# Modulation loads issued by GpSimd into three buffers, and twelve output-projection chunks of layer 0 computed in split form

## The chip, the cores and the metric

The kernel runs on one core of a Trainium2 chip. The metric is the device time of one execution in microseconds (us), taken as the median of three runs. TensorE (PE in the profile) multiplies matrices, VectorE (DVE) and ScalarE (ACT) do elementwise work, GpSimd (POOL) does a few small operations, and SyncE (SP) issues the transfers between the memory of the chip (HBM) and the core's own memory (SBUF). TensorE writes into PSUM, a small accumulation memory.

## The reference

A decoder trunk of two layers works on 256 tokens of width 2048, all in float32. Each layer mixes tokens and then applies a gated feed-forward network (FFN). Both are modulated by a vector `c`:

```python
for l in range(DEPTH):                       # DEPTH = 2
    mod = silu(c) @ w_mod[l] + b_mod[l]      # 2048 x 12288 weights, one row of c
    shift1, scale1, gate1, shift2, scale2, gate2 = split(mod, 6)
    h = rms_norm(x, norm1_gain[l]) * (1 + scale1) + shift1
    x = x + gate1 * hybrid_token_mixer(h, ..., w_in[l], ..., w_out[l])
    h = rms_norm(x, norm2_gain[l]) * (1 + scale2) + shift2
    x = x + gate2 * ((silu(h @ w_gate[l]) * (h @ w_up[l])) @ w_down[l])
return rms_norm(x, final_norm_gain)
```

The token mixer multiplies `h` by `w_in` (2048 x 4888 columns), gives the columns to three mixers and multiplies their joined output `mix` (256 x 2048) by `w_out` (2048 x 2048). The three mixers are GLA (gated linear attention, which uses a small 16 x 256 gate weight `w_gk`), a sliding-window attention (SWA) and a gated delta rule (GDN). The FFN is 5632 wide. All weights are read from HBM once, about 600 MB.

## The kernel before

**The large products.** `stream` (L293) walks over jobs. One job is one chunk of 128 rows of a weight matrix and up to 1024 of its columns: SP loads it (L323, 512 KB), and it is multiplied with the transposed activations of both token blocks of 128. A job has one of two forms. In the *whole* form the float32 weights go to TensorE as they are; the profile shows two matmul records for each product of 128x128 with 128x512. In the *split* form ScalarE copies the weights into a rounded part `wh` (L330), VectorE subtracts it to get the rest `wl` (L331), and TensorE does three products: high by high, high by low, low by high (L358). Activations are split too, by `split` (L386). `WHOLE_IN`, `WHOLE_A` and `WHOLE_OUT` say which chunks are whole. `WHOLE_OUT[0] = (0, 1, 2, 3)` makes all four groups of four chunks of layer 0's output projection whole; in layer 1 all are split. Chunk `k` belongs to group `k // 4`: 0 is GLA, 1 and 2 are SWA, 3 is GDN. `to_mix` (L489) puts a mixer's output into tiles of the pool `hm`, and `split_mix` (L520), called ahead of `gla`, splits those groups that are not whole. The output projection runs first over chunks 4 to 15 for both halves of the columns (24 jobs) and then, when GLA is done, over chunks 0 to 3 (8 jobs).

**The modulation.** The products with `c` are not done by TensorE. `mod_segment` (L201) cuts the modulation into segments; a step of one loads 128 rows of `w_mod` by SP (L220), and VectorE multiplies them by one value of `c` for each partition and adds them to an accumulator (L223). Once all steps of a segment are in, `finish` (L228) sums the accumulator over its partitions with TensorE (L238 for gates, L248 for shifts and scales). The first segments, shift1 and scale1 of layer 0 ("early"), are 512 columns wide and land in scratch tiles `g`. All others are 1024 wide: 320 loads of 512 KB into the two buffers `mraw` of the pool `modp`; the two accumulators `acc` are cleared by GpSimd (L212) and get their bias row by a transfer of SP (L213). `finish` of a gate borrows `mraw` buffers as well (L233).

**The order.** `tick` (L273) is called after each job and starts modulation steps at a rate that the constants `RATE_...` set (2.0 steps to a job in layer 0's output projection, 0.4 in its FFN). What the text writes down in this order is then put into one queue for each engine by a scheduler with costs of its own, which pulls work forward where its operands and buffers allow it; each engine runs its queue in order. So a transfer on SP that waits for a buffer holds back all transfers behind it. Other users of GpSimd's queue are `rsqrt` (L408), used by the norms and the mixers, the sinks of SWA (L891), the memsets, and the copy L218, which holds the first modulation load behind the second norm of a layer.

**Small tiles.** `ones` (L163) is a float32 tile of ones that a copy on ScalarE turns into `ones_r` of the type that the fast products use; `ones` itself is used at L594. `load_small` (L464) loads the gate weights `wgk` at the start of each layer, together with other small weights.

## Time and profile before

| what | before |
|---|---|
| median of 3 runs | 2582.44 us (2582.32 to 2587.12) |
| the profiled execution, its own time | 2585.34 us |
| its span, first to last instruction | 2583.5 us |
| busy: TensorE, VectorE, ScalarE, GpSimd | 94%, 66%, 41%, 2% of the span |
| moved by transfers | 600.79 MB, 233 GB/s over the span |
| mean granted TensorE clock | 0.986 of full speed |

The time of the profiled execution is its span and what lies around it. A row of instructions gives the line of the kernel, the engine, the operation, output<-inputs by the program's names, the shapes and the count, then the busy time and the mean duration in ns, then the engine's idle time just before these instructions and what ended it. Matmuls overlap, so that the mean duration of one (some 390 ns) is longer than the step from one to the next. SPq stands for SP's transfer queue. A row of the chain of waits gives the start, the duration and what the chain ran through at that time. `mraw` and `raw` are the buffers of modulation and of weights.

### The profile page before, as it was taken

To read this page: it belongs to the slowest core of one execution; us is meant where nothing else is said; L and a number is where in the kernel's file an instruction comes from. 1 tells how busy PE (TensorE), PEld (TensorE's weight loads), DVE (VectorE), ACT (ScalarE), POOL (GpSimd) and SP (SyncE) were. 2 spreads that over 40 slices of the span, in tenths; PEclk is the share of its full clock that TensorE was granted. 3 is DMA by queue.
4 is the path that set the end of the run, shared out by engine and by line. 5 is a ranking of instruction groups with operands and counts; after the bars stand their busy time and mean duration, and the time that the engine had idled before them with its cause. 6 is when DMAs were issued, how large, how long until landed. Compare 5 with 4: busy or idle time off the path is not lost.

```text
span 2583.5 us, 30803 instructions
## 1 busy us (share of the span) xinstructions
PE 2432.7 (94%) x11164; PEld 1884.1 (73%) x11164; DVE 1714.4 (66%) x2171; ACT 1053.5 (41%) x1548; POOL 58.2 (2%) x117
## 2 busy tenths in 40 slices
PE   4999998889999988999999999999999999999998
PEld 2555785447878767788877878877778878888876
DVE  6767867576675777657578785888664575544555
ACT  2203443124444333344335454564644434344443
POOL 1000000000000000000000000000000000000000
PEclk9999999989999999999999999999999999999999
DMA  9996538777778888868687861675676686666654
GB/s 341 368 322 204 180 114 282 258 231 268 261 259 260 283 268 274 292 193 286 223 277 261 281 192 50 214 232 192 212 256 193 200 286 195 188 191 188 189 184 155
DMA packets 190033, 600.79 MB, mean 233 GB/s; under 512 B 21628, under 2 KB 26268, under 8 KB 189496
## 3 DMA queue, kind: packets, MB, share of 16 engines
q1 hardware_dynamic: 189880, 598.81, 70.7%
q8 instruction: 88, 1.44, 0.2%
q14 instruction: 65, 0.53, 0.1%
HBM read 596.63 MB, written 2.10 MB: 232 GB/s over the span
## 4 chain that ended last, share of the span: by engine, by line
PE 57%; DMA 20%; DVE 10%; issue 8%; ACT 4%; POOL 1%; SPq 1%; DVEq 0%; ACTq 0%; POOLq 0%
PE acc L358 48%; DMA mraw<-in_w_mod 13%; DVE wl L331 4%; DMA raw<-in_w_down 3%; DMA raw<-in_w_in 2%; DVE acc L223 2%; ACT wh L330 1%; PE mm L403 1%; PE ga L895 1%; DMA raw<-in_w_up 1%; PE mm L678 1%; PE mm L685 1%; PE ga L916 1%; DMA raw<-in_w_gate 1%; PE fin L248 1%
## 5 line engine op out<-in xcount | busy, mean ns | idle before, releaser
L358 PE MATMUL acc<-wh,hm 128*128 128x512 f32 (+3 forms) x4872 | 1339.2, 389 | 20.9 <-DVE xs L931 4.7
L330 ACT ACTIVATE wh<-raw 128x1024 fp32r<-128x1024 f32 (+3 forms) x669 | 684.7, 1025 | 985.8 <-PE acc L358 548.9
L331 DVE TENSOR_TENSOR wl<-raw,wh 128x1024 fp32r<-128x1024 f32 (+3 forms) x669 | 785.2, 1179 | 446.6 <-ACT wh L330 444.5
L358 PEld LDWEIGHTS acc<-wh,hm 128*128 128x128 f32 x4872 | 892.0, 189 | 215.8 <-issue 25.5
L358 PE MATMUL acc<-wl,hm 128*128 128x512 f32 (+3 forms) x2484 | 792.3, 394 | 12.2 <-DVE wl L331 9.7
L223 DVE SCALAR_TENSOR_TENSOR acc<-mraw,c_act,acc 128x1024 f32<-128x1024 f32 x320 | 410.3, 1282 | 225.2 <-DMA mraw<-in_w_mod 222.9
L358 PEld LDWEIGHTS acc<-wl,hm 128*128 128x128 f32 x2484 | 458.4, 190 | 124.1 <-DVE wl L331 22.3
L358 PE MATMUL acc<-wh,ahl 128*128 128x512 f32 x560 | 158.4, 397 | 0.0
L358 PEld LDWEIGHTS acc<-wh,ahl 128*128 128x128 f32 x560 | 105.8, 189 | 24.5
L358 PE MATMUL acc<-wl,ahl 128*128 128x512 f32 x280 | 90.8, 398 | 7.2 <-DVE wl L331 7.2
L223 DVE SCALAR_TENSOR_TENSOR g<-g,c_act,g 128x512 f32<-128x512 f32 x128 | 88.7, 747 | 12.6 <-DMA g<-in_w_mod 12.4
L358 PE MATMUL acc<-wh,b 128*128 128x512 f32 (+2 forms) x184 | 74.7, 545 | 2.2 <-ACT b L447 2.1
L358 PE MATMUL acc<-wl,b 128*128 128x512 f32 (+2 forms) x176 | 67.1, 518 | 2.6 <-DVE g L969 2.6
L358 PEld LDWEIGHTS acc<-wl,ahl 128*128 128x128 f32 x280 | 52.2, 189 | 23.1 <-DVE wl L331 11.3
L358 PE MATMUL acc<-raw,b 128*128 128x512 f32 (+2 forms) x176 | 67.6, 524 | 0.0
L358 PEld LDWEIGHTS acc<-wh,b 128*128 128x128 f32 x184 | 35.2, 197 | 30.8 <-issue 23.1
L358 PEld LDWEIGHTS acc<-wl,b 128*128 128x128 f32 x176 | 32.8, 192 | 29.2 <-issue 20.3
L416 ACT ACTIVATE acc<-xs 128x512 f32<-128x512 f32 x32 | 19.0, 595 | 85.7 <-DVE xs L931 85.7
L447 ACT ACTIVATE b<-mm,mod,mod 128x128 f32<-128x128 f32 x24 | 9.2, 461 | 109.7 <-DVE mod L256 92.1
L358 PEld LDWEIGHTS acc<-raw,b 128*128 128x128 f32 x176 | 33.5, 195 | 26.7 <-issue 21.7
L929 DVE TENSOR_TENSOR acc<-acc,gate 128x512 f32<-128x512 f32 x64 | 43.0, 695 | 10.3 <-PE acc L358 10.2
L358 PE MATMUL acc<-raw,hm 128*128 128x512 f32 x88 | 41.7, 598 | 1.4 <-ACT acc L416 1.4
(314 smaller groups left out, 1645.8 us busy)
## 6 DMA issues: line engine op xcount, KB each, us to landing
mraw<-in_w_mod SPq DMA_DIRECT2D x320, 512.0 KB
raw<-in_w_down SPq DMA_DIRECT2D x176, 512.0 KB
raw<-in_w_gate SPq DMA_DIRECT2D x160, 512.0 KB
raw<-in_w_up SPq DMA_DIRECT2D x160, 512.0 KB
raw<-in_w_in SPq DMA_DIRECT2D x72, 512.0 KB
g<-in_w_mod SPq DMA_DIRECT2D x128, 256.0 KB
raw<-in_w_out SPq DMA_DIRECT2D x43, 512.0 KB
raw<-in_w_in SPq DMA_DIRECT2D x32, 264.0 KB
```

The costliest lines, as they stand in the source:

```text
L223: V.scalar_tensor_tensor(acc, raw[:, a], c_act[:, i + a:i + a + 1], acc, ALU.mult, ALU.add)
L248: TE.transpose(ps[:, i * P:(i + 1) * P], acc[:, (j + i) * P:(j + i + 1) * P], ident)
L330: A.activation(wh[:, :width], raw[:, :width], AF.Copy)
L331: V.tensor_tensor(wl[:, :width], raw[:, :width], wh[:, :width].bitcast(F32), ALU.subtract)
L358: TE.matmul(ps[blk, j][:, :segs[j][2]], xa, parts[j][part], start=i == 0 and n == 0, stop=last and n == len(terms) - 1)
L403: TE.transpose(ps[:, j * P:(j + 1) * P], src[:, j * P:(j + 1) * P], ident)
L416: A.activation(scr[0]() if junk is None else junk, xs[:, blk, j * 512:(j + 1) * 512], AF.Square, accum_out=ssq[blk][:, j:j + 1])
L678: TE.matmul(ps[:, s], LT[blk][:, s], Tm[blk][:, s], start=True, stop=True)
L685: TE.matmul(ps[:, s], U[blk][:, s], m1[:, s], start=True, stop=True)
L895: TE.matmul(ps[:, j * nk:(j + 1) * nk], qT[rows, i + j], kT[rows, g, :nk], start=True, stop=True)
L916: TE.matmul(ps[:, j * 64:(j + 1) * 64], pT[:, j * nk + kb * P:j * nk + (kb + 1) * P], kv[kb][:, P + g * 64:P + (g + 1) * 64], start=kb == ...
L929: V.tensor_tensor(ps, ps, need(gate_row, (l, part, j)), ALU.mult)
```

## The change

GpSimd, and no longer SP, issues the bias rows and the loads of the 1024-column modulation segments; the early segments stay with SP. The pool of these loads has three buffers in place of two. In layer 0's output projection the groups 1, 2 and 3 (twelve chunks, 24 jobs) take the split form, and group 0 stays whole. The tile `ones` and the copy that made `ones_r` from it go away: GpSimd writes the ones straight into `ones_r`, and L594 reads that tile as float32. The gate weights are loaded at the start of `gla` into a tile of GLA's own pool.

```diff
-WHOLE_OUT = ((0, 1, 2, 3), ())
+WHOLE_OUT = ((0,), ())
...
-    modp = ctx.enter_context(tc.tile_pool(name="modp", bufs=2))
+    modp = ctx.enter_context(tc.tile_pool(name="modp", bufs=3))
...
-    ones = tl(kp, [P, P], "ones")
-    G.memset(ones, 1.0)
     ones_r = tl(kp, [P, P], "ones_r", F32R)
-    A.activation(ones_r, ones, AF.Copy)
+    G.memset(ones_r.bitcast(F32), 1.0)
...
                 G.memset(st["acc"][:, :width], 0.0)
-                SY.dma_start(st["acc"][0:1, :width], b_mod[l:l + 1, c0:c0 + width])
+                issue = SY if early else G
+                issue.dma_start(st["acc"][0:1, :width], b_mod[l:l + 1, c0:c0 + width])
...
-            SY.dma_start(raw, w_mod[l, i * P:(i + n) * P, c0:c0 + width]
-                         .rearrange("(a p) n -> p a n", p=P))
+            (SY if early else G).dma_start(raw, w_mod[l, i * P:(i + n) * P, c0:c0 + width]
+                                           .rearrange("(a p) n -> p a n", p=P))
...
     def load_small(l):
         small_t[l] = tl(kp, [P, SMALL_W], "small")
         SY.dma_start(small_t[l], small[l][:, 2 * KD:])
-        wgk_t[l] = tl(kp, [16, 256], "wgk")
-        SY.dma_start(wgk_t[l], w_gk[l])
...
                         TE.matmul(ps[:, n:n + 1], sq[:, c, blk * P:(blk + 1) * P],
-                                  ones[:, 0:1], start=True, stop=True)
+                                  ones_r[:, 0:1].bitcast(F32), start=True, stop=True)
...
     def gla(l, pool, qk_tok, v_tok, zg, lr):
 
+        wgk = tl(pool, [16, T], "wgk", bufs=1)
+        SY.dma_start(wgk, w_gk[l])
...
-            TE.matmul(ps[:, blk * T:(blk + 1) * T], lrT[:, blk * P:(blk + 1) * P], wgk_t[l],
+            TE.matmul(ps[:, blk * T:(blk + 1) * T], lrT[:, blk * P:(blk + 1) * P], wgk,
```

More of the change, by code (lines that the diff above doesn't have):

```diff
@@ L458, in trunk @@
     scr = [None, None]
-    small_t, wgk_t = {}, {}
+    small_t = {}
     gains = tl(kp, [P, DEPTH, 2 * KD], "gains")
```

## The prediction

> **What bounds the kernel now.** I read the page first: busy shares, then the chain of waits by engine and by line.
>
> ```profile
> span 2583.5 us, 30803 instructions
> ...
> PE 2432.7 (94%) x11164; PEld 1884.1 (73%) x11164; DVE 1714.4 (66%) x2171; ACT 1053.5 (41%) x1548; POOL 58.2 (2%) x117
> ...
> PE 57%; DMA 20%; DVE 10%; issue 8%; ACT 4%; POOL 1%; SPq 1%; DVEq 0%; ACTq 0%; POOLq 0%
> PE acc L358 48%; DMA mraw<-in_w_mod 13%; DVE wl L331 4%; DMA raw<-in_w_down 3%; DMA raw<-in_w_in 2%; DVE acc L223 2%; ACT wh L330 1%; PE mm L403 1%; PE ga L895 1%; DMA raw<-in_w_up 1%; PE mm L678 1%; PE mm L685 1%; PE ga L916 1%; DMA raw<-in_w_gate 1%; PE fin L248 1%
> ```
>
> TensorE is nearly always busy, and yet 13% of the chain runs through modulation loads. These two fit together only if a busy TensorE is not always a TensorE at full pace, so I next counted its large products in three stretches of the FFNs: layer 0 with modulation, layer 1 with a little of it, layer 1 with none.
>
> ```profile
> 590.00:1100.00 510.00, 478.90 (x2032) 380.58 (x2031) 0.99 0.82 275
> 1850.00:2130.00 280.00, 270.86 (x1177) 219.67 (x1176) 1.00 0.74 238
> 2150.00:2550.00 400.00, 394.79 (x1717) 321.53 (x1717) 1.00 0.61 189
> ```
>
> The columns are the stretch, its length, TensorE's busy time on L358 (records), weight loads, granted clock, transfer share, GB/s. Without modulation the pace is 1717/400 = 4.29 records to a us. At it the 2032 of the first stretch take 473.4 us instead of 510: **36.6 us are lost there**, and 280 - 1177/4.2925 = 5.8 us in the second. The clock is 0.99 to 1.00, so it is not the clock.
>
> What the first stretch waits for is in its groups, its waits on SP, and the chain.
>
> ```profile
> L331 DVE TENSOR_TENSOR wl<-raw,wh 128x1024 fp32r<-128x1024 f32 x170 | 206.1, 1222 | 61.5 <-ACT wh L330 60.9
> L330 ACT ACTIVATE wh<-raw 128x1024 fp32r<-128x1024 f32 x170 | 179.9, 1060 | 295.9 <-PE acc L358 72.9 <-DMA raw<-in_w_down 68.9 <-DMA raw<-in_w_up 65.0
> L223 DVE SCALAR_TENSOR_TENSOR acc<-mraw,c_act,acc 128x1024 f32<-128x1024 f32 x96 | 123.2, 1284 | 95.9 <-DMA mraw<-in_w_mod 95.3
> ```
>
> ```profile
> SPq L323 <- DVE wl L331: 308.8, 161, 4.2
> SPq L220 <- DVE acc L223: 33.7, 30, 2.1
> SPq L220 <- DMA mraw<-in_w_mod: 21.8, 15, 3.0
> ```
>
> There is a ring of waits here. VectorE stands 95.3 us in front of L223, because a modulation load was issued late, behind a weight load that waited for its own buffer (308.8 us on SP). While it stands, `wl` of the next weights waits, their buffer comes free late, and the next weight load is late. The other way round, SP stands 55.5 us (33.7 + 21.8) on modulation loads, with weight loads behind them. One weight load comes every 510/170 = 3.00 us; at full pace it would be 473.4/170 = 2.78.
>
> Before that, layer 0's output projection shows the same in a stronger form.
>
> ```profile
> 481.93 5.50 DMA mraw<-in_w_mod
> 487.46 1.30 DVE acc L223
> ...
> 511.26 4.29 DMA mraw<-in_w_mod
> 515.65 1.30 DVE acc L223
> 517.08 1.09 PE fin L248 x4
> ...
> 521.50 20.97 PE acc L358 x48
> ```
>
> ```profile
> 517.08 1.09 PE L248 MATMUL fin<-consts,acc 128*128 128x128 f32 x4 [5.88 <-DVE acc L223]
> ```
>
> From 481.93 to 517.08 the chain alternates between a load and L223. Its links start 6.8, 4.9, 6.0, 6.6 and 5.0 us apart, the first at 481.93 and the last at 511.26: 29.3 us for five, 5.9 us for a link. A link is two loads, since there are two buffers: 2.9 us for one load. TensorE runs ahead and then stands 5.88 us. After that whole products run without a gap: 20.97/48 = 0.437 us for a record.
>
> **The change part by part.**
>
> *GpSimd's queue and the third buffer, in the FFNs.* The wait of VectorE (95.3 us, 0.56 us for each of 170 weight loads) and the hold on SP (55.5 us, 0.33 us) both lie in the cycle of a weight buffer, and there are three of those. Taking both away shortens the period by (0.56 + 0.33)/3 = 0.30 us, more than the 0.22 us that are there to be had. So the bound is 36.6 us. I take three quarters of it, 27 us, since the loads still share the transfers (0.82 of their time in use at 275 GB/s), and 4 of the 5.8 us in layer 1. What is late next is the weight load itself.
>
> *The split of twelve chunks.* A whole job has 8 records of 0.437 us: 3.50 us. A split one has 12 products, and their step comes from a gapless piece of the chain:
>
> ```profile
> 1112.83 50.38 PE acc L358 x222
> ```
>
> That is 0.227 us each, 2.72 us a job, 0.77 us saved; 24 jobs give 18.5 us, and the stall of 5.88 us can go too: 24.4 us at most. Against it stand VectorE's new work, 24 times 1.22 us (L331) and six tiles in `split_mix` like this row,
>
> ```profile
> L338 DVE TENSOR_TENSOR hm<-raw,hm 128x512 fp32r<-128x512 f32 x32 | 20.9, 688 | 10.8 <-ACT hm L337 10.7
> ```
>
> 29.3 + 4.1 = 33.4 us, and what VectorE has there now:
>
> ```profile
> 393.00:556.00 163.00, 147.16 (x558) 77.27 (x559) 110.49 (x147) 34.91 (x74) 5.89 (x5) 0.98 0.82 272
> ```
>
> ```profile
> L223 DVE SCALAR_TENSOR_TENSOR acc<-mraw,c_act,acc 128x1024 f32<-128x1024 f32 x48 | 61.6, 1282 | 40.9 <-DMA mraw<-in_w_mod 40.7
> ```
>
> (third column: VectorE 110.49 us, fourth: ScalarE 34.91.) 110.5 + 33.4 = 143.9 of 163 us: it fits only because the third buffer takes away most of the 40.7 us of waiting. With GLA's chain of small steps in the same stretch I let it fill to 94%: 143.9/0.94 = 153 us, so 10 us are won. The bounds are a gain of 24.4 us and a loss of 8 (rival 3). ScalarE gets 24 times 1.06 and six times some 0.6 us on 34.91 in 163; that is hidden by its idle time. A whole weight lands in one of nine buffers (`raw`, `wh`, `wl` in turn), a split one in one of three; this cover goes, and the weights of this stage become as exposed as those of the FFN.
>
> *Layer 1's input projection* has both kinds of load as well:
>
> ```profile
> ACT wh L330 <- DMA raw<-in_w_in: 40.8, 28, 5.2
> DVE acc L223 <- DMA mraw<-in_w_mod: 12.9, 14, 1.8
> ```
>
> (1380 to 1500 us.) The wait for weights is the larger one and the transfers have no room for it; of the 12.9 us I take 3 (bounds 0 and 12.9).
>
> *What GpSimd's queue costs.* No transfer of GpSimd is in this trace. Its issue lies between what SP takes and the longest instruction that GpSimd has:
>
> ```profile
> L220 SPq DMA_DIRECT2D mraw<-in_w_mod x320: 327/328/1439, 160.9 to 2122.4; - x160
> ```
>
> ```profile
> L408 POOL TENSOR_TENSOR grs<-gss,half 128x4 f32<-128x4 f32 x8 | 11.3, 1418 | 159.8 <-DVE gss L508 159.8
> L408 POOL TENSOR_TENSOR qkrs<-qkss,half 128x16 f32<-128x16 f32 x2 | 5.8, 2920 | 167.7 <-DVE qkss L596 167.7
> ```
>
> 0.33 us to 2.92 us; I take 1 us, nearer to the short end, since no data passes through GpSimd. A load that lands 0.7 us later than before is covered by the third buffer: it is asked for one period (2.9 us in the fastest stage) sooner. But GpSimd now waits in order for the L223 that frees the buffer, with the memset of the next accumulator, the sinks of SWA (L891) and `rsqrt` behind it; for these wait VectorE's steps in the mixers and norms. The ten rows above and the four norms inside the layers, 14 places, may each come one issue late: 14 times 0.33 is 4.6, times 2.92 is 41; mixers run beside other products, so I take 4 us.
>
> *Small edits.* The gate weights move past the weight loads on SP to the start of GLA, with no queue but SP's to pass. They are needed at the second of these:
>
> ```profile
> 405.27 0.60 PE L747 MATMUL ga<-consts,hm 128*128 128x128 f32 x4
> ...
> 412.32 1.13 PE L761 MATMUL ga<-wgk,lrT 16*128 16x256 f32 x4
> ```
>
> 7 us after GLA's first step; a load of 512 KB takes 3.5 to 5.5 us (chain above), so these 7 us hide a 16 KB one. Without the cover it costs a load, 5.5 us at most, in each layer. The memset in place of memset and copy lies ahead of the first products, behind the first loads: nothing.
>
> *The sum:* -27 - 4 - 10 - 3 + 4 = **-40 us**. The profiled execution took 2585.34 us with a span of 2583.5; it would take 2545.3, with a span of 2543.5. It lies 2.9 us above the median of the runs shown, 2582.44, so against that I predict 2542.
>
> **The rivals.**
>
> *1. The transfers set the pace anyway.* All loads go through the same 16 engines, in use for 0.82 of the time with modulation and 0.61 without. If a weight load is late because the engines are full, a second queue only swaps the order. Against it: 18% of their time is free while VectorE waits. Then the FFN gives 5 us, the output projection 5 and GpSimd costs 4: 2576. The Trainium skill speaks for this one (DMA: Bandwidth & Descriptors, Issuing engines are not separate DMA queues): issuing from several engines only saves the time of issuing. By it alone, the gain would be next to nothing; what it leaves out is one queue waiting for a buffer with the other's work behind it, which the 55.5 us show here.
>
> *2. Slower: weights lose the queue to modulation.* On one queue a weight load waits only for what was issued before it. With two, a modulation load issued after it takes half of the engines while both are under way. One load at the stage's rate takes 0.524 MB / (275/0.82 GB/s) = 1.56 us. The cycle of a weight buffer was to become 0.89 us shorter (0.56 + 0.33), so this decides from 0.89 us on; weights that land a full load later make the period (1.56 - 0.89)/3 = 0.22 us longer, and 170 of them 38 us. With no gain elsewhere and the 4 us for GpSimd: 2624. Against it: at most three modulation loads can be under way, and their rate is set by the program.
>
> *3. VectorE becomes the bound in layer 0's output projection.* If the transfers still make it wait, 33.4 us of new work meet a free time of 163 - 110.5 - 40.7 = 11.8, and 21.6 us do not fit. If the third buffer takes back a third of the wait, 13.6 us, then 8 us are lost instead of 10 won: 2560.
>
> *4. GpSimd is slow to issue.* At 2.92 us a load the three buffers give (5.9 + 2.92)/3 = 2.94 us for one, where two buffers now give 2.9: nothing is won in the output projection; FFN 13 us, less 8 for `rsqrt`: 2577. The Trainium skill warns of it (SBUF — State Buffer, SBUF: two separate sides): GpSimd cannot write the descriptors of its transfers while VectorE runs a copy or the like that uses both its port pairs, so that 0.62 us become 3.1; by its figures a load behind such an instruction comes 2.5 us later. VectorE's main rows here, L331 and L223, have two inputs each and are not of that kind; by the page such a lock would concern little here but this row and its likes:
>
> ```profile
> L441 DVE TENSOR_SCALAR s<-xs,rms 128x512 f32<-128x512 f32 x16 | 7.5, 481 | 0.8 <-POOL rms L408 0.7
> ```
>
> **How the numbers follow.** The forecast gets 0.48, rival 1 0.15, rival 2 0.13, rival 3 0.14, rival 4 0.10. A measurement of this kernel can tell about 0.2%, 5 us, from no change. Forecast and rival 3 are faster; rivals 1 and 4 lie at the edge of that, half of 1 and 0.03 of 4 beyond it; rival 2 is slower, with 0.03 of rival 4 if the issue is longer still. Faster 0.72, same 0.12, slower 0.16. The low end has nearly all bounds: 36.6 + 5.8 + 24.4 + 12.9 = 79.7 gained, 2503. The high end takes in rivals 1, 3 and 4 and the mild part of 2: 2596. The forecast's own range is 2515 to 2562.
>
> **What would show it.**
>
> ```profile
> DVE acc L223 <- DMA mraw<-in_w_mod: 222.9, 170, 4.0
> ```
>
> Right: this wait falls under 100 us; the modulation stretch of layer 0's FFN at over 4.2 records to a us; waits on SP for L223 gone; in the output projection of layer 0 rows of `wh` and `wl` with 128x512 products and no stall of some 6 us before `fin`; GpSimd's waits before `rsqrt` a few us longer. Wrong: the same waits under `raw` instead of `mraw` (rivals 1, 2), VectorE over 95% busy from 393 us on (3), GpSimd's transfers far apart with their buffers free (4).

## The result, and the profile after

The changed kernel took 2690.8 us (median of 4 runs, 2688.0 to 2697.4) beside 2583.6 for the kernel before on the same chip: a ratio of 1.0416 with a 95% interval of 1.0394 to 1.0439. It is slower by 107 us; 2542 was predicted, and the range ended at 2596. The profiled execution took 2689.4 us, with a span of 2687.6.

The page of the changed kernel: busy shares, and the groups that answer to those of before.

```profile
span 2687.6 us, 31258 instructions
...
PE 2461.7 (92%) x11260; PEld 1922.1 (72%) x11260; DVE 1746.2 (65%) x2201; ACT 1080.8 (40%) x1576; POOL 238.8 (9%) x457
...
L222 DVE SCALAR_TENSOR_TENSOR acc<-mraw,c_act,acc 128x1024 f32<-128x1024 f32 x320 | 409.8, 1281 | 213.3 <-DMA mraw<-in_w_mod 203.0
L219 POOL DMA_DIRECT2D mraw<-in_w_mod x320 | 170.8, 534 | 1133.8 <-DVE acc L222 905.1
...
mraw<-in_w_mod POOLq DMA_DIRECT2D x320, 512.0 KB, 5.5
raw<-in_w_down SPq DMA_DIRECT2D x176, 512.0 KB, 4.5
```

Lines have moved by one or two: L222, L219 and L357 are L223, L220 and L358 of before. GpSimd issues a load in 0.534 us. VectorE's wait for loads, 222.9 us before, is 203.0: the third buffer and the queue of its own took a tenth of it away.

TensorE's large products in the three FFN stretches, as before (stretch, length, busy time and records on L357, weight loads, clock, transfer share, GB/s), placed the same time after the norm that opens each FFN to within a few us:

```profile
625.00:1135.00 510.00, 469.15 (x1947) 367.40 (x1946) 0.98 0.79 271
1928.00:2208.00 280.00, 263.00 (x1111) 211.55 (x1112) 0.98 0.72 232
2228.00:2628.00 400.00, 394.80 (x1716) 321.21 (x1715) 1.00 0.60 187
```

Without modulation the pace is that of before (1716 records to 1717). With it, 2032 have become 1947 and 1177 have become 1111: the pace fell from 3.98 to 3.82 a us where it was to rise over 4.2.

To see where all of the time went I cut the span at six instructions of GpSimd that every version has, `rsqrt` in the mixers (`qkrs`) and in the norms (`rms`). These are they in the timeline of the changed kernel (start, duration, instruction, idle time before it and its cause):

```profile
298.39 2.93 POOL L407 TENSOR_TENSOR qkrs<-qkss,half 128x16 f32<-128x16 f32 x1 [6.37 <-DVE qkss L593]
611.01 0.55 POOL L407 TENSOR_TENSOR rms<-ss,half 128x1 f32<-128x1 f32 x1 [11.21 <-DVE ss L421]
1422.22 0.56 POOL L407 TENSOR_TENSOR rms<-ss,half 128x1 f32<-128x1 f32 x1 [27.97 <-DVE ss L421]
1595.64 2.93 POOL L407 TENSOR_TENSOR qkrs<-qkss,half 128x16 f32<-128x16 f32 x1 [69.08 <-DVE qkss L593]
1904.73 0.56 POOL L407 TENSOR_TENSOR rms<-ss,half 128x1 f32<-128x1 f32 x1 [11.56 <-DVE ss L421]
2666.06 0.56 POOL L407 TENSOR_TENSOR rms<-ss,half 128x1 f32<-128x1 f32 x1 [602.81 <-DVE ss L421]
```

Differences of their starts are the stages. The table gives them in us for the versions that the next section needs; "SP" and "GpSimd" say who issues the 1024-column loads. The marks lie where mixers, output projection and FFN partly overlap, so a few us can move from one stage to its neighbour.

| version (profiled execution) | start, input proj. 0 | mixers and w_out 0 | FFN 0 | input proj. 1 | mixers and w_out 1 | FFN 1 |
|---|---|---|---|---|---|---|
| before | 252.9 | 319.8 | 793.1 | 153.3 | 303.6 | 743.5 |
| small edits alone, SP | 250.3 | 320.3 | 789.4 | 156.0 | 303.3 | 745.9 |
| before, GpSimd issues | 277.9 | 338.3 | 808.5 | 180.5 | 303.7 | 757.5 |
| changed kernel | 298.4 | 312.6 | 811.2 | 173.4 | 309.1 | 761.3 |
| changed, SP | 248.2 | 321.4 | 766.0 | 161.0 | 304.8 | 744.4 |
| changed, SP, no split | 246.9 | 298.8 | 766.8 | 160.6 | 303.8 | 743.5 |
| changed, no split | 300.4 | 324.0 | 813.9 | 171.7 | 307.2 | 760.0 |
| changed, ScalarE issues | 323.2 | 319.1 | 800.4 | 185.1 | 300.7 | 749.8 |
| changed, start held | 268.9 | 305.3 | 810.8 | 170.6 | 307.0 | 756.8 |
| 64-column loads, GpSimd | 280.8 | 298.2 | 754.7 | 150.8 | 304.1 | 746.0 |
| 64-column loads, SP | 247.6 | 289.3 | 748.2 | 153.2 | 303.8 | 743.2 |

The profiled execution of "changed, SP, no split" took 2539.8 us, 7.8 below the median of its runs, so its stages are a little short as a whole.

Against before, the changed kernel loses 45 us by the first mark, wins 7 in layer 0's mixers and output projection, and loses 18 in each FFN and 20 in layer 1's input projection.

### The profile page after: what moved, and what is told of

The parts are those of the page before. It is cut to its first block, busy times and chain, and to the rows that moved or that the text cites. A ratio compares the mean times of both kernels' runs of the same rounds, so it can differ in the third digit from the quotient of the medians.

```text
span 2687.6 us, 31258 instructions
## 1 busy us (share of the span) xinstructions
PE 2461.7 (92%) x11260; PEld 1922.1 (72%) x11260; DVE 1746.2 (65%) x2201; ACT 1080.8 (40%) x1576; POOL 238.8 (9%) x457
## 5 line engine op out<-in xcount | busy, mean ns | idle before, releaser
L357 PE MATMUL acc<-wh,hm 128*128 128x512 f32 (+3 forms) x5000 | 1385.8, 391 | 32.8 <-ACT s L1133 10.3
L330 DVE TENSOR_TENSOR wl<-raw,wh 128x1024 fp32r<-128x1024 f32 (+3 forms) x693 | 814.8, 1180 | 520.3 <-ACT wh L329 518.1
L329 ACT ACTIVATE wh<-raw 128x1024 fp32r<-128x1024 f32 (+3 forms) x693 | 710.4, 1026 | 1069.8 <-PE acc L357 662.9
L357 PEld LDWEIGHTS acc<-wh,hm 128*128 128x128 f32 x5000 | 930.4, 192 | 228.9 <-ACT s L1133 13.0
L357 PE MATMUL acc<-wl,hm 128*128 128x512 f32 (+2 forms) x2516 | 808.9, 395 | 47.2 <-DVE wl L330 41.3
L357 PEld LDWEIGHTS acc<-wl,hm 128*128 128x128 f32 x2516 | 469.9, 192 | 162.2 <-DVE wl L330 64.4
L222 DVE SCALAR_TENSOR_TENSOR acc<-mraw,c_act,acc 128x1024 f32<-128x1024 f32 x320 | 409.8, 1281 | 213.3 <-DMA mraw<-in_w_mod 203.0
L219 POOL DMA_DIRECT2D mraw<-in_w_mod x320 | 170.8, 534 | 1133.8 <-DVE acc L222 905.1
L357 PE MATMUL acc<-wh,ahl 128*128 128x512 f32 x560 | 157.4, 395 | 0.0
L357 PEld LDWEIGHTS acc<-wh,ahl 128*128 128x128 f32 x560 | 105.6, 189 | 24.4
L222 DVE SCALAR_TENSOR_TENSOR g<-g,c_act,g 128x512 f32<-128x512 f32 x128 | 89.8, 745 | 8.7 <-DMA g<-in_w_mod 8.4
L357 PE MATMUL acc<-wl,ahl 128*128 128x512 f32 x280 | 90.0, 395 | 1.0 <-DVE wl L330 1.0
L357 PE MATMUL acc<-wh,b 128*128 128x512 f32 (+2 forms) x184 | 76.5, 554 | 10.5 <-DMA wh<-in_w_in 8.1
L357 PE MATMUL acc<-wl,b 128*128 128x512 f32 (+2 forms) x176 | 69.0, 531 | 8.6 <-DMA wl<-in_w_in 5.8
L357 PE MATMUL acc<-raw,b 128*128 128x512 f32 (+2 forms) x176 | 71.2, 547 | 4.3 <-DVE b L968 2.4
L407 POOL TENSOR_TENSOR rms<-ss,half 128x1 f32<-128x1 f32 x10 | 6.4, 642 | 707.4 <-DVE ss L421 706.2
L357 PEld LDWEIGHTS acc<-wh,b 128*128 128x128 f32 x184 | 35.2, 201 | 40.2 <-issue 29.0
L357 PEld LDWEIGHTS acc<-wl,ahl 128*128 128x128 f32 x280 | 52.8, 189 | 14.2 <-DVE wl L330 1.9
L357 PEld LDWEIGHTS acc<-wl,b 128*128 128x128 f32 x176 | 33.7, 196 | 37.3 <-issue 21.8
L357 PEld LDWEIGHTS acc<-raw,b 128*128 128x128 f32 x176 | 34.0, 198 | 34.9 <-issue 27.0
L210 POOL MEMSET acc<- 128x1024 f32 x20 | 19.1, 953 | 357.5 <-PE fin L247 331.3
```

Of the source, the lines that this page charges most:

```text
L210: G.memset(st["acc"][:, :width], 0.0)
L219: (SY if early else G).dma_start(raw, w_mod[l, i * P:(i + n) * P, c0:c0 + width] .rearrange("(a p) n -> p a n", p=P))
L222: V.scalar_tensor_tensor(acc, raw[:, a], c_act[:, i + a:i + a + 1], acc, ALU.mult, ALU.add)
L329: A.activation(wh[:, :width], raw[:, :width], AF.Copy)
L330: V.tensor_tensor(wl[:, :width], raw[:, :width], wh[:, :width].bitcast(F32), ALU.subtract)
L357: TE.matmul(ps[blk, j][:, :segs[j][2]], xa, parts[j][part], start=i == 0 and n == 0, stop=last and n == len(terms) - 1)
```

## The experiments

### The parts, one by one

**The change with SP issuing.**

```diff
-                issue = SY if early else G
-                issue.dma_start(st["acc"][0:1, :width], ...
+                SY.dma_start(st["acc"][0:1, :width], ...
...
-            (SY if early else G).dma_start(raw, ...
+            SY.dma_start(raw, ...
```

> The changed kernel with one part undone: SP again issues the modulation's loads and bias rows; the third buffer, the split chunks and the small edits stay. Theory A (GpSimd's own queue lets the 1024-column loads run ahead of their place: 35 of them, 18 MB, go into the start, where the transfers are full, and bursts of them delay the weights later): the time comes back to 2555 to 2590 us, and the last early modulation load is issued near 143 us, not 190. Theory B (the third buffer lets the loads run ahead, whoever issues them): it stays within 20 us of 2691. Theory C (the split chunks cost it, since their weights have three buffers instead of nine): 2650 or more, and the output projection of layer 0 is the place.

Measured: 2568.1 us, ratio to the kernel before 0.9942 [0.9918, 0.9966]. All of the loss and more hangs on who issues.

**The kernel before with GpSimd issuing**, and nothing else: the opposite edit, on two buffers and without the split.

> The kernel before with one part done alone: GpSimd issues the modulation's loads and bias rows, still into two buffers. Theory A: 2660 to 2700 us, most of the loss, with the last early load near 185 us. Theory B: 2570 to 2590, since two buffers hold the loads back. Theory C: 2570 to 2590.

Measured: 2695.5 us, 1.0433 [1.0392, 1.0474]. The issue alone makes the whole slowdown. The stages share it out a little otherwise: with two buffers the first mark is 25 us later than before, with three 45.

**The kernel before with the split alone** (`WHOLE_OUT = ((0,), ())`).

> The kernel before with the twelve chunks of layer 0's output projection split, and nothing else. Theories A and B: 2565 to 2590 us, the split is not what costs. Theory C: 2620 or more.

Measured: 2583.2 us, 1.0013 [0.9993, 1.0033]: no difference.

**The small edits alone**: the change with SP issuing, two buffers and no split.

> The kernel before with only the small edits of the change: ones set straight by GpSimd without ScalarE's copy, and the gate weights loaded in GLA's pool. My prediction counted them at nothing, so 2580 as before. The gain of the version with SyncE issuing (2568) would then be the third buffer's and the split's together. If this is at 2570 or below, the gain is theirs instead, by the other order in which the work then falls.

Measured: 2583.0 us, 1.0002 [0.9985, 1.002]: nothing, as predicted.

**The small edits and the third buffer**, SP issuing, no split.

> The small edits with a third buffer for the 1024-column loads, SyncE issuing, no split. The small edits alone made no difference (1.0002), nor did the split (1.0013). If the third buffer makes the gain of the version with all three and SyncE issuing (0.9942), this is at 2566 to 2572; if it needs the split with it, 2578 to 2585. My prediction gave the third buffer 27 and 4 us in the feed-forwards.

Measured: 2547.5 us, 0.9864 [0.9837, 0.9892]. This is below both outcomes that I had written down, and the fastest version that computes everything: 1.4% faster than the kernel before. I had not thought that the split takes something away.

**The changed kernel without the split**, GpSimd issuing.

> The changed kernel without the split of the twelve w_out chunks: GpSimd issuing, three buffers, small edits. With SyncE issuing the split cost 20 us (2547.5 without, 2568 with). If it costs the same here, 2665 to 2680; if the split gains behind late loads as my prediction had it (10 us), 2695 to 2705; the layer-0 output projection's own stage tells the same (108 us in the changed kernel, from GLA's last norm to the next).

Measured: 2703.6 us, 1.0494 [1.0464, 1.0523]: with GpSimd issuing the split gains, as my prediction had it.

The ratios side by side:

| | SP issues | GpSimd issues |
|---|---|---|
| two buffers | 1.0002 | 1.0433 |
| two buffers, split | 1.0013 | not run |
| three buffers | 0.9864 | 1.0494 |
| three buffers, split | 0.9942 | 1.0416 |

(GpSimd with two buffers was run without the small edits, and so was SP with two buffers and the split.) The third buffer gains 1.4% with SP; with GpSimd it gains nothing (the intervals of 1.0433 and 1.0494 overlap). The split costs 0.8% with SP and three buffers and gains 0.8% with GpSimd. GpSimd's issue costs 4.3 to 6.3% everywhere. So the parts of this change are not terms of a sum.

### The start

Two rows of the changed kernel, all loads of the modulation in its first 300 us (line, engine, count: shortest, median and longest duration in ns, first and last start):

```profile
L219 SPq DMA_DIRECT2D g<-in_w_mod x128: 327/328/1386, 4.3 to 190.5; - x128
...
L219 POOL DMA_DIRECT2D mraw<-in_w_mod x36: 527/528/693, 2.7 to 291.5; - x36
```

And the same with SP issuing:

```profile
L218 SPq DMA_DIRECT2D mraw<-in_w_mod x35: 327/328/432, 160.9 to 295.3; - x35
...
L218 SPq DMA_DIRECT2D g<-in_w_mod x128: 327/328/654, 4.1 to 142.7; - x128
```

On SP the 1024-column loads stand behind the 128 early ones, without which layer 0 can't begin: the first goes out at 160.9 us. On a queue of its own it goes out at 2.7 us, before the first early load, and the last early load is issued 48 us later. Three things can do that. Transfers are full there (in both versions their share is 0.95 to 1.02 over the first 100 us), and VectorE works on the new loads first:

```profile
0.00:50.00 50.00, 0.00 (x0) 0.00 (x0) 10.24 (x8) 0.00 (x0) 5.60 (x11) 1.00 0.96 350
50.00:100.00 50.00, 0.00 (x0) 0.00 (x0) 17.90 (x15) 1.26 (x2) 6.32 (x12) 0.97 1.02 383
```

These are the instructions on `mraw` in stretches of the changed kernel; the third busy time is VectorE's, 23 instructions in 100 us where the version with SP has none.

The third is GpSimd's own queue. The accumulators of the early segments are cleared by GpSimd (L210), and these memsets now stand behind 1024-column loads that wait for VectorE to free a buffer. SP can't issue an early segment's bias row (L212) before the memset, and the early loads stand behind it. SP's waits in the first 200 us, the changed kernel and then the version with SP:

```profile
SPq L212 <- POOL g L210: 19.9, 5, 9.0
...
SPq L211 <- POOL g L210: 2.5, 3, 1.0
```

With ScalarE issuing (below) this wait is 2.0 us and the start is later still, so it is not the whole of it.

**The start held**: one column of the last early accumulator is copied by GpSimd into the first 1024-column buffer, so that this load, and all behind it, wait for the early ones.

```diff
+            if early:
+                gate_on[:] = [acc[:, 0:1]]
+            elif gate_on:
+                G.tensor_copy(raw[:, 0:1], gate_on.pop())
```

> The changed kernel with one copy of one column on GpSimd ahead of the first 1024-column load, which reads the accumulator of the last early segment: this load and all behind it wait until the early segments are summed. Theory A: the 45 us of the start come back, 2635 to 2655 us, and the rest of the loss stays. If the start is only slow because of GpSimd's transfers as such or the small edits, it stays near 2690.

Measured: 2653.9 us, 1.0266 [1.0221, 1.031]; the first 1024-column load at 150.6 us, the last early one at 142.1. It wins back 37 us, 29.5 of them by the first mark. There 20.7 us against SP remain, and some 86 us of the whole.

**The start held and no split.**

> The version with the start held (2654), without the split. If split and issue are independent costs, 2630 to 2640, and then the start (37 us), the split (20 us) and the later stages' transfers (some 75 us) add up to what the changed kernel loses against three buffers and SyncE (143 us): 2547 + 75 to 85.

Measured: 2674.3 us, 1.0376 [1.0336, 1.0416], and not 2630 to 2640: the split gains 1.1% here. Issue and split are not independent, and the parts don't add up.

### The bytes, or the issue

**64 columns instead of 1024**, in the changed kernel and in the version with SP: each load brings a sixteenth, and VectorE reads it sixteen times over. The modulation is not computed.

```diff
-            (SY if early else G).dma_start(raw, w_mod[...c0:c0 + width] ...
+                G.dma_start(raw[:, 0, :64], w_mod[l, i * P:(i + 1) * P, c0:c0 + 64])
+                cols = [raw[:, 0, :64].unsqueeze(1).to_broadcast([P, width // 64, 64])]
```

> The changed kernel, but each 1024-column load brings 64 columns only (32 KB instead of 512 KB) and VectorE's accumulation reads these sixteen times over: the modulation is not computed. The order on the engines stays nearly that of the changed kernel (2029 of 2202 VectorE instructions in the same order), and 157 MB of the 600 MB are not moved. Theory 'transfers': GpSimd's issue costs 120 us only through when its 160 MB move, so without them this agrees with the same cut under SyncE's issue within 15 us, both below 2560. Rival 'issue': GpSimd's instructions, or the order they give VectorE, cost wherever the bytes go: then this stays 60 us or more above the SyncE version.

> The same 64-column loads with SyncE issuing: the modulation is not computed. It shows what the transfers of the modulation cost at all in the version with SyncE issuing (2568): by the DMA share of 0.6 to 0.9 in the feed-forward I expect 20 to 70 us less, 2500 to 2550; 'transfers' and 'issue' differ in how far the GpSimd version of the same cut lies above this one: under 15 us, or 60 and more.

Measured: 2557.9 us (0.9902 [0.9872, 0.9931]) and 2502.9 us (0.9691 [0.9662, 0.972]). The gap of 123 us between the two issuers becomes 55: neither of the two outcomes I had set apart, and the stages say why. FFN 0, input projection 1 and FFN 1 together: GpSimd lost 74.5 us to SP with full loads (45.2 + 12.4 + 16.9) and loses 7 with small ones (6.5 - 2.4 + 2.8). At the start it lost 50 and still loses 33. The small loads also change the order a little (2029 of 2202 instructions of VectorE stand in the same order), and the early loads show the start with the bytes of the 1024-column loads gone:

```profile
L220 SPq DMA_DIRECT2D g<-in_w_mod x128: 327/328/744, 4.3 to 180.5; - x128
```

The last early load is issued at 180.5 us, though the small 1024-column loads take next to nothing. So most of the delay at the start is not in the bytes. In the first 200 us SP stands 61.4 us waiting for VectorE's early accumulations (29.1 in the version with SP and 64 columns) and 21.9 us for GpSimd's memsets (3.0 there): VectorE's work on the new loads and GpSimd's queue are both in it, and no run parts the two.

**The same with the start held.** Again the modulation is not computed.

> The 64-column loads by GpSimd (2558, the modulation is not computed) with the start held by the one-column copy. If the 55 us by which that lies above SyncE's version of the same cut (2503) are the start alone, this comes to 2503 to 2520. If something of GpSimd's issue costs throughout, it stays above 2535.

Measured: 2534.5 us, 0.9818 [0.9789, 0.9846], between the two outcomes. The last early load is back at 142.4 us, and 23 of the 55 us are won. The first mark is still 12.8 us later than with SP, layer 0's mixers and output projection take 7.6 longer: the held loads come right after the hold, into the work of the input projection. That reading is argued, not tested.

### Is it GpSimd?

**ScalarE issuing** (`A` in place of `G` in both places).

> The changed kernel with ScalarE instead of GpSimd issuing the 1024-column loads: also another queue than the weights', but on an engine with other work in order (the weights' halves), so that a load waits for its place. Theory 'place': first 1024-column load after 120 us, no burst of more than 8 in 25 us in layer 0's feed-forward, and under 2640; ScalarE waiting for a free buffer ahead of a weight's half is the price and may take some of it back. Rival 'second queue': two queues beside each other slow the weights wherever the loads stand: 2670 or more.

Measured: 2695.4 us, 1.0432 [1.0399, 1.0465], the same as with GpSimd. The queues of that version (packets, MB, share of 16 engines):

```profile
q1 hardware_dynamic: 143760, 430.94, 49.0%
q10 hardware_dynamic: 46120, 167.87, 18.6%
```

and its loads in the first 330 us:

```profile
L219 SPq DMA_DIRECT2D g<-in_w_mod x128: 327/371/709, 13.5 to 218.1; - x128
...
L219 ACTq DMA_DIRECT2D mraw<-in_w_mod x36: 334/335/406, 0.7 to 318.0; - x36
```

So a loss of this size needs neither GpSimd nor its software queue; a second queue, whoever fills it, makes it. The start is later still (first mark 323), the FFNs are a little better. My theory that ScalarE's own work would hold the loads in place fell: the first one went out at 0.7 us.

### The later stages

In the same 510 us of layer 0's FFN the versions compared here have exactly 96 accumulations L222 each, that is, 96 loads used. Three buffers with SP:

```profile
560.00:1070.00 510.00, 486.41 (x2082) 389.36 (x2081) 0.99 0.83 281
```

64-column loads by GpSimd:

```profile
593.00:1103.00 510.00, 495.49 (x2140) 399.31 (x2140) 1.00 0.63 192
```

against 1947 records in the changed kernel, and 2097 in the version that differs from it in the issuer alone. With the same number of loads, a second queue costs 135 to 150 records, 31 to 35 us at 4.29 a us, and cutting the bytes gives them back and more. The waits in this stretch show where it arrives. The changed kernel:

```profile
DVE acc L222 <- DMA mraw<-in_w_mod: 81.2, 51, 4.0
...
PEld acc L357 <- DVE wl L330: 33.9, 36, 3.3
...
PE acc L357 <- DVE wl L330: 18.8, 24, 2.9
```

Three buffers with SP:

```profile
DVE acc L221 <- DMA mraw<-in_w_mod: 76.0, 53, 3.3
...
PEld acc L356 <- DVE wl L329: 9.1, 13, 1.1
PE acc L356 <- DVE wl L329: 3.6, 8, 0.7
```

VectorE waits a little longer for loads in the changed kernel: 81.2 us, against 76.0 here and 64.3 in the version that differs in the issuer alone, while 31 to 35 us are lost. But TensorE's weight loads wait 33.9 us for `wl` in the one and 9.1 in the other, its products 18.8 and 3.6 (the two run side by side, so they don't add up), 3.3 us at the longest against 1.1. So the sum of VectorE's waiting makes at most half of the difference; the delays reach TensorE, past the three weight buffers, in the one and mostly not in the other. Two explanations were tried.

**Loads in single file.** The last step of a gate (L233, L234) borrows two of the three `mraw` buffers until TensorE gets to it. Then each load has to wait for the accumulation just before it; in the changed kernel the built order does so for 72 of the 320 loads. VectorE in such a stretch:

```profile
764.07 1.28 DVE L222 SCALAR_TENSOR_TENSOR acc<-mraw,c_act,acc 128x1024 f32<-128x1024 f32 x1 [1.98 <-DMA mraw<-in_w_mod]
765.27 2.40 DVE L330 TENSOR_TENSOR wl<-raw,wh 128x1024 fp32r<-128x1024 f32 x2
769.68 1.28 DVE L222 SCALAR_TENSOR_TENSOR acc<-mraw,c_act,acc 128x1024 f32<-128x1024 f32 x1 [2.01 <-DMA mraw<-in_w_mod]
770.88 1.22 DVE L330 TENSOR_TENSOR wl<-raw,wh 128x1024 fp32r<-128x1024 f32 x1
775.67 1.29 DVE L222 SCALAR_TENSOR_TENSOR acc<-mraw,c_act,acc 128x1024 f32<-128x1024 f32 x1 [3.57 <-DMA mraw<-in_w_mod]
```

Each load costs VectorE 2 to 3.6 us, with `wl` behind it. To take it away, that last step got a buffer of its own, and the loads two that nothing else uses:

```diff
-    modp = ctx.enter_context(tc.tile_pool(name="modp", bufs=3))
+    modp = ctx.enter_context(tc.tile_pool(name="modp", bufs=2))
...
-                    t = tl(modp, [P, 2, 512], "mraw", F32R)
+                    t = tl(modp, [P, 2, 512], "fint", F32R, bufs=1)
```

With SP issuing:

> The changed kernel with SyncE issuing, and the gates' last step (the copies at line 233 and 234) in a buffer of its own, so that the loads keep two buffers always. Theory 'held buffers': the gates' last step holds two of the three buffers for 40 to 190 us each time, and the loads then go one at a time through the third, each landing about 4 us after its issue with VectorE waiting 2 us for it. Then this gains over SyncE issuing with three shared buffers (2568): 36 such loads by 2 us are up to 72 us of VectorE's wait, of which perhaps 5 to 15 us reach TensorE: 2553 to 2563. Rival: two buffers are the limit of before again, or TensorE was not kept waiting in those stretches: 2568 to 2580.

and with GpSimd issuing:

> The same buffer for the gates' last step, but with GpSimd issuing as in the changed kernel (2691). In the changed kernel 72 loads have only the buffer that the load just before them gave back. If those single-file loads make the loss in layer 0's feed-forward, this gains 30 us or more: 2660 or less. If the bursts make it ('place'), it stays within 15 us of 2691.

Measured: 2573.6 us (0.9947 [0.9925, 0.9969]) and 2688.3 us (1.0399 [1.0362, 1.0436]), both in total like the same version with three shared buffers. In the second no load waits for the one just before it any more, and FFN 0 still takes 810 us, so taking the single file away wins nothing there. The edit leaves the loads two buffers, though, and with SP that costs 23.6 us in FFN 0 (789.6 us against 766.0), which the stages ahead of it give back in part; with GpSimd FFN 0 takes 808.5 us with two shared buffers and 811.2 with three. Single file is not the cause, unless the lost buffer hid its gain.

**Loads in bunches.** Held only by free buffers and free accumulators, up to 11 of GpSimd's loads go out within 25 us of FFN 0, and four gaps of 41 to 109 us lie between; with SP issuing (three buffers and split) it is up to 8, and two gaps over 40 us, of 54 and 82. The bunches are also written into VectorE's queue, whose order was built together with the issue: between two accumulations of FFN 0 there stands at most one weight split (L330) in 92 of 127 places in the changed kernel, and in 61 with SP. Three versions were to hold the loads to a place. In two of them ScalarE copies a column of each weight chunk as it comes, and GpSimd copies it, two or five chunks later, into the load's buffer before the load:

```diff
+            if not early and len(pace) > PACE:
+                G.tensor_copy(raw[:, 0:1], pace[-1 - PACE])
...
+        def mark(tile):
+            c = 1 + len(pace) % 7
+            pace.append(eps_all[:, c:c + 1])
+            A.activation(pace[-1], tile[:, 0:1], AF.Copy)
```

> The changed kernel, GpSimd issuing, but each 1024-column load is held to its place among the weights: ScalarE copies one column of each weight chunk as it turns it into its half (some 570 tiny copies, about 0.2 us each, on an engine that is 43% busy), and GpSimd copies that column, of the chunk two before, into the load's buffer before it issues the load. Theory 'place': GpSimd's loads cost time because nothing but free buffers holds them, so that in layer 0's feed-forward 8 to 10 of them fall into 25 us (69 to 94 matmuls there against 105 to 112) and then none for 75 to 100 us. Held, the time should come to that with SyncE issuing, 2568, within 15 us; the first 1024-column load after 120 us; no stretch of 25 us with more than 8 loads. Rival 'second queue': two queues share the transfers worse, or GpSimd's issues themselves disturb VectorE, wherever they stand: then it stays at 2640 or above.

> As the held version before it (2780), but GpSimd's load is held to the weight chunk five before instead of two, some 9 us earlier at 2.9 us a chunk. In the held version VectorE waited 438 us for these loads, 2.4 us each time, with the weights' subtractions behind it. If the hold came too late there and loads in their place are no dearer by GpSimd than by SyncE, VectorE's wait falls under 150 us and the time to 2570 to 2610. If GpSimd's issue itself, or its queue, is what costs, the wait may fall but the time stays above 2650.

Measured: 2780.5 us (1.0758 [1.0713, 1.0803]) and 2804.5 us (1.0867 [1.0825, 1.0909]). The longest waits of the first:

```profile
POOL mraw L218 <- ACT eps L318: 1397.0, 201, 66.1
DVE acc L225 <- DMA mraw<-in_w_mod: 438.2, 186, 7.2
```

The loads were spread, and VectorE waits twice as long for them as in the changed kernel. It did so with the hold five chunks back as well (431.5 us), so my reading that the hold came too late there fell with it. These two say only that a later load is dearer; the bunches remained open.

In the third, GpSimd works for some us ahead of each load of the FFNs, on top of the held start, with the order of VectorE's instructions kept (2191 of 2202; the constants of `RATE_FFN` are changed in the third digit, to tell the FFNs from the other stages):

```diff
+            if not early and rate[1] in RATE_FFN:
+                one = ones_r.bitcast(F32)[:, :24]
+                G.tensor_tensor(raw[:, :24], one, one, ALU.pow)
```

> The version with the start held (2654), and in the two feed-forwards GpSimd works some 4 us (a power over 24 columns, at 2.9 us for 16 columns by the row of line 407) ahead of each 1024-column load, so that no two loads follow each other in under about 4.8 us: at most 5 in 25 us instead of 8 to 11. The order of the instructions on the other engines stays (2191 of 2202 on VectorE). Theory 'bunches': the loads' bunching fills the transfers in some stretches and leaves them half idle in others; spread, layer 0's feed-forward falls from 800 us to 760 to 775, layer 1's from 746 to about 735, and the whole to 2605 to 2630. Rival 'two queues share': the weights lose to a second queue at any pace: the feed-forward stays at 790 or more, and the 4 us of added delay make VectorE wait longer.

Measured: 3016.2 us, 1.1671 [1.1645, 1.1697]. FFN 0 takes 1069.6 us in place of 810.8. GpSimd's added row over the whole run, and VectorE's wait over that stage:

```profile
L222 POOL TENSOR_TENSOR mraw<-ones_r 128x24 f32<-128x24 f32 x119 | 559.0, 4697 | 252.4 <-DVE acc L229 227.5 <-PE fin L244 18.6 <-DVE mod L262 4.7
```

```profile
DVE acc L229 <- DMA mraw<-in_w_mod: 354.4, 91, 8.1
```

and the wait of VectorE in the same stage with the start held and no added work:

```profile
DVE acc L226 <- DMA mraw<-in_w_mod: 96.7, 65, 3.6
```

VectorE waits 257.7 us more, and the stage is 258.8 us longer: between these two versions each us that VectorE stands in front of a load is a us of the stage. As a test of the bunches it failed by its own delay: no experiment spread the loads without making them late.

What speaks against the bunches is a count. I cut layer 0's FFN into stretches of 25 us and counted accumulations and large products in each. In stretches with 6 to 8 loads, the version with SP and three buffers makes 105.1 records on average (14 stretches), the changed kernel 93.0 (8); with 3 to 5 loads it is 99.9 (10) and 95.3 (9). So a stretch with as many loads gets less done beside a second queue, which bunches over 25 us don't give by themselves; closer bunches within a stretch are not ruled out. This is a comparison within two traces, not an experiment.

**Do weights land later beside a second queue?** The traces answer this for FFN 0. The semaphore updates give each load's time from its issue to its landing (the last update of its semaphore before that semaphore's next load). Over the 246 to 248 weight loads of 512 KB it is 4.9 us on average in the changed kernel, 4.9 in both versions with SP and three buffers, 5.0 in the kernel before and 4.7 there with GpSimd issuing. ScalarE, which takes each weight first, waits 165.2 us for weights in the 510 us of the changed kernel, and 163.9 in those of the kernel before. So with two queues a weight load, once issued, is as fast as with one.

**Where it stands.** Shown: the slowdown comes from issuing on a second queue, the total doesn't depend on which engine issues, 29.5 of the 45 us lost at the start come back when the loads are held until the early ones are through, and the loss of the later stages goes when their bytes go. Not shown: how the bytes and the times of the loads make that loss together. Weights that lose time on the way because the engines are shared have the landing times against them. Loads that come at other times than SP's order gave them fit the built order of VectorE; that order alone costs little, since the version with 64-column loads has it too (at most one split in 96 of 127 places) and loses 7 us in these stages. No run tests this reading by itself.

## Why the prediction was wrong

**The ring of waits, and what to take out of it (-27 and -4 us).** The ring was there, and the size was near, but for another version: with SP issuing, the third buffer shortens FFN 0 from 789.4 us (small edits alone) to 766.8, by 22.6, and FFN 1 by 2.5. That is in part luck, since in the stretch of 510 us VectorE's wait fell only from 95.3 us to 76.0. The queue of its own was to take away the hold on SP, 0.33 of the 0.89 us. It gave nothing and cost 47 us (813.9 against 766.8, three buffers, no split). The step that failed is "taking both away": VectorE's wait stayed (81.2 of the 95.3 us), and I priced SP's hold of 55.5 us on modulation loads as pure loss. SP's waits for the modulation are gone in the changed kernel, as expected, and with them went an order in which loads could not run ahead of the weights. That it is this order which FFN 0 misses is argued; the start shows it.

**What GpSimd's queue costs (+4 us).** This is the term that sank the forecast: done alone, the move to GpSimd costs 4.3%, some 112 us, and not 4. The issue takes 0.534 us, inside my bounds of 0.33 and 2.92. Among those who wait behind GpSimd I priced only `rsqrt`, and not the memsets of the early accumulators, for which SP stands 19.9 us at the start. Above all I did not ask what these loads had waited behind on SP. The trace of before had the answer in a row that I quoted for another purpose, the issues of L220 from 160.9 us on: for 160 us nothing but SP's order held them. By the first mark the changed kernel had lost 45 us.

**Rival 2, weights lose the queue to modulation (2624).** It had the right sign, and 0.13, but not the mechanism: weights that land later were to make it, and they land in the same 4.9 us. Its other sign, ScalarE's waits under `raw` in place of `mraw`, did not come either (163.9 us before, 165.2 after). It priced FFN 0 at 38 us over before; it was 18 over before and 45 over the same kernel with SP. It had no start, no layer 1, and so ended 67 us short. Against it I wrote that the rate of the loads is set by the program; the changed kernel's first 100 us and the stretches without a load show that on a queue of its own it is set by free buffers and accumulators.

**Rival 1, the transfers set the pace anyway (2576).** The rule of the Trainium skill that spoke for it (DMA: Bandwidth & Descriptors, Issuing engines are not separate DMA queues) held as far as it goes: no version gained by the second queue, from GpSimd or from ScalarE, and I was wrong to set 55.5 us against it. That section also says that transfers from several engines interleave on the same 16 DMA engines, and the same page's section Queues, rings and completion order that each of these takes packets from its queues in turn. This would be rival 2's mechanism; no trace here shows the turns themselves, the landing times show no loss by them, and the slowdown of 4 to 6% is in neither place.

**The split (-10 us).** In the changed kernel it gains 0.8% (1.0494 without, 1.0416 with), and the stage of mixers and output projection 11.3 us: the size I gave. With SP and three buffers the same edit lengthens that stage by 22.6 us. There TensorE's busy time falls only from 287.0 us to 283.6, where I had 18.5 us for the saving alone, and its idle time grows from 11.8 us to 37.8. The cover that I noted as lost may be a part of that. In the output projection, 473.67 to 569.61 us of the version with SP and split, the first row of TensorE is

```profile
L356 PE MATMUL acc<-wh,hm 128*128 128x512 f32 x118 | 42.0, 467 | 12.6 <-ACT wh L328 12.6
```

and without the split, from 458 to 545 us,

```profile
L356 PE MATMUL acc<-raw,hm 128*128 128x512 f32 x63 | 29.4, 594 | 0.3 <-ACT acc L414 0.3
```

From GLA's last norm to the next norm it takes 95.9 us with the split and 88.3 without: some 8 us of the 22.6 lie there, the others already ahead of it, in the mixers beside which the first chunks run; what makes those I have not taken apart. The third buffer itself gave this stage 21.5 us (320.3 to 298.8), which my sum had booked for the split.

**Layer 1's input projection (-3 us).** It became 20 us longer with GpSimd and 7 to 8 with SP and three buffers, and 2.7 longer with the small edits alone (156.0). I had looked only at what its waits could give back.

**Small edits (0) and rivals 3 and 4.** The small edits made no difference (1.0002). In the changed kernel's output projection (stretch, length, busy time of TensorE, its weight loads, VectorE, ScalarE and GpSimd, clock, transfer share, GB/s)

```profile
523.04:611.01 87.97, 71.66 (x245) 43.64 (x243) 68.83 (x85) 25.38 (x49) 17.55 (x30) 0.94 0.77 271
```

VectorE was busy 68.8 of 88.0 us, and 129 of the last 163 us of the stage, so rival 3 did not occur. GpSimd issued in 0.534 us, so neither did rival 4, and the lock that was named beside it does not show.

## What to carry to other kernels

A queue that holds transfers back is also an order: before moving loads to another queue, look in the trace for what they wait behind, and ask what they will run ahead of once that is gone, and what will stand behind them on the new engine. A loaded queue that stalls on buffers may need a buffer more and not a queue more: here the third buffer alone, with SP still issuing, was worth 1.4%, and the queue cost 4 to 6%. Test the parts of a change in pairs: the split changed sign with the issuer, and the third buffer's gain was there with one issuer and not with the other.

## What the runs showed of the hardware

A second queue filled by ScalarE's hardware issue (0.335 us each) cost as much in total as one filled by GpSimd (0.534 us). I had expected the issuer to matter.

A weight load of layer 0's FFN took 4.9 us from issue to landing on average whether the modulation loads came on the same queue or on a second one.

TensorE's clock fell where it was kept waiting. Layer 0's FFN in the version with GpSimd's added work:

```profile
590.00:1100.00 510.00, 340.76 (x1182) 256.67 (x1182) 0.82 0.53 171
```

With TensorE busy on large products 341 of 510 us the granted clock is 0.82, against 0.98 and 0.99 in the stretches of layer 0's FFN where it was busy over 460. A product by `wh` took 442 ns on average there and 398 in the changed kernel, which points to a cost of the wait on top of itself; how much of it is the clock is not shown. The Trainium skill (TensorE: Matmul & The Clock Gate, Part 1: The HAM clock gate) describes a clock that drops when TensorE is idle; the trace agrees in direction.
